# A two-layer decoder trunk on one core: q beside k, v of four heads and z of two groups as matmuls with 512 moving columns

## The chip, the cores and the metric

The kernel runs on one core of one Trainium2 chip. The metric is the device time of one execution in microseconds (us).

## The reference

Two layers over 512 tokens of width 1024, in float32. Each layer is a half-weighted SwiGLU, a token mixer and a second half-weighted SwiGLU, each behind an RMS norm and added to `x`. Layer 0 mixes by causal attention of 8 heads of width 128 (blocks of 256 keys, so that at 512 tokens every past block is chosen), layer 1 by a Mamba-2 mixer of 8 groups with 4 heads each.

```
for i in range(2):
    x = x + 0.5 * swiglu(rms_norm(x), gate[i], up[i], down[i])     # 1024 -> 2816 -> 1024
    h = rms_norm(x)
    x = x + (attention(h) if i == 0 else mamba2(h))
    x = x + 0.5 * swiglu(rms_norm(x), gate2[i], up2[i], down2[i])

attention(h): q, k, v = h @ w_qkv                    # 1024 -> 3 * 1024
              q, k = rope(rms_norm(q) * gq), rope(rms_norm(k) * gk)   # norms per head
              o = softmax(causal(q k^T / sqrt(128))) v;  return o @ w_o
mamba2(h):    z, xbc, dt = h @ w_in;  xbc = silu(conv4(xbc));  y = ssd(xbc, dt) + d * xs
              y = group_rms_norm(y * silu(z));  return y @ w_out
```

## The kernel before

**Tiling.** `x` lies transposed in SBUF: 8 tiles of 128 features by 512 tokens. Every float32 operand is split into a high and a low part (`high`, on ACT, and `low`, on DVE), and `mm3` makes one product out of three matmuls: high by high, high by low, low by high. A weight comes in pieces of up to 128x2048 (`wraw`, four buffers, loaded by SP's queue), and `halve_weights` and `halve_low` turn each piece into units of 128x512 (`whi` on ACT, `wlo` on DVE, eight buffers of each).

**Shapes.** In the feed-forward parts, the mixer's `pin` and the output projections the weight is stationary and 512 tokens move. q, k and v of attention and the mixer's z are made token-major instead: 128 tokens of `h` (`xhi`, `xlo`) are stationary and the weight's columns move. `token_major` (L751) does so with 256 columns (two heads) and puts two token tiles side by side into one bank of PSUM; the mixer's loop at L1022 does the same for z of one group.

**Stages.** `attention` (L600) has four passes `c` of two heads, each with a piece for q, k and v (`wqkv[c, what]`). `roped` (L622) takes one bank: squares on ACT, the power -0.5 on POOL, the scaling and the sine product `ropeb` on DVE, the cosine product and the sum `ropea` on POOL, four transposes `ptr` on PE, and the halves `qkhi`, `qklo`. `head` (L661) makes scores `psc`, the softmax, transposes `ppt` and the product with v `po`; `project` (L725) adds the output projection `pwo`. `rope_tables` (L568) makes the sines and cosines; `prepare` spawns it at the start of attention. `mamba` (L793) runs its groups one after the other: `conv_tile` (`pin`), four `chunk`s of 128 tokens (`pxt`, `py`, `pst`), z (`pz`, gated by `gate`), `gated_norm` (transposes `pyt`, halves `yhi`, `ylo`) and, after groups 2, 4 and 7, a projection `pout`.

**Order.** Each of these is a Python generator that hands its instructions to `Scheduler` (L137). It keeps a planned clock for each engine, gives every instruction a planned length (`Op.cost`), and always issues the one that can begin first; `main` (L1076), which holds the big matmuls, comes last where several can. The result is one fixed list for each engine, and on the chip each engine works its list off in order. `pieces` (L332) lists the weights in the order of use, with planned times that set when a unit is halved.

Of the kernel before, what the change touches and what calls it, by code (L numbers as in the profile page):

```python
# [17 lines left out]
FR = mybir.dt.float32r  # L18
# [18 lines left out]
FIRST = (("w", 0), ("x", 0), ("x", 1), ("w", 1), ("x", 2), ("x", 3), ("w", 2), ("x", 4), ("x", 5), ("w", 3), ("x", 6), ("x", 7))  # L37

# [246 lines left out]
def trunk(ctx, tc, xT, pos, consts, cols, rows, wgu, wd, wqkv, wo, win, wdt, wout, outT):  # L285
# [48 lines left out]
    def piece(src, n, us):  # L334

        pieces.append((src, n, us))

    for l in range(2):
        for i in (2 * l, 2 * l + 1):
            if i == 1:  # L340
                for c in range(4):
                    for w in range(3):
                        if c == 3 and w == 2:
                            piece(wo[0], 2048, 1.36)
                        piece(wqkv[c, w], 2048, 0.72)
                for c in range(1, 4):
                    piece(wo[c], 2048, 1.36)
            if i == 3:
                piece(wdt, 256, 1.36)
                for g in range(G):  # L350
                    piece(win[g, 0], 2048, 2.73)
                    piece(win[g, 1], 2048, 2.73)
                    piece(win[g, 2], 2048, 0.72)
                    if g in (2, 4, 7):
                        for o in range(2):
                            piece(wout[{2: 0, 4: 1, 7: 2}[g], o], 2048, 2.73)
                for o in range(2):
                    piece(wout[3, o], 2048, 2.73)
            for hf in range(2):
                for j in range(HALF):  # L360
                    piece(wgu[i, hf * HALF + j], 2048, 2.73)
                for n in range(KT):
                    piece(wd[i, hf, n], HALF * 128, 2.73)
    length = {0.72: 11.5, 1.36: 5.5, 2.73: 10.9}
    raws, begun, units = {}, {}, {}
    needed, at = [], 0.0
    for src, n, us in pieces:
        needed.append(at)
        at += length[us] * n / 2048 if us != 0.72 else 11.5
    used = [0]  # L370

    def load_weights():
        for p in range(1, len(pieces)):
            src, n, _ = pieces[p]
# [130 lines left out]

    def residual(n, ps, scale, done):
# [7 lines left out]
    def ffn(i, nrm, done):  # L514
# [16 lines left out]
        for hf in range(2):  # L531
            h = {}
# [35 lines left out]
    def rope_tables():  # L568
        posf = yield tiny("posf", TT)
        yield V.tensor_copy(posf, posi)  # L570
        big = yield [slot(nm) for nm in ("ang", "angq", "sin", "cos")]
        ang, q, s, c = (b[:, :256] for b in big)
# [15 lines left out]
        for nm, g in (("q", q_gain), ("k", k_gain)):  # L588
            ta, tb = yield [slot(nm + o) for o in ("cos", "sin")]
            ta, tb = (t.rearrange("p (i d) -> p i d", d=128) for t in (ta, tb))  # L590
            for o in range(2):
                same = g[:, None, 64 * o:64 * o + 64].to_broadcast([128, TT, 64])
                other = g[:, None, 64 - 64 * o:128 - 64 * o].to_broadcast([128, TT, 64])
                yield GP.tensor_tensor(ta[:, :, 64 * o:64 * o + 64], c.rearrange("p (i d) -> p i d", d=64), same, op=OP.mult)
                yield GP.tensor_tensor(tb[:, :, 64 * o:64 * o + 64], s.rearrange("p (i d) -> p i d", d=64), other, op=OP.mult)
            op = GP.tensor_scalar(tb[:, :, 0:64], tb[:, :, 0:64], -1.0, None, op0=OP.mult)
            yield op.frees(big[2], big[3]) if nm == "k" else op
            tabs.append((ta, tb))

    def attention(nrm, done):  # L600
# [6 lines left out]
        heads_left = [2] * 4  # L607
# [14 lines left out]
        def roped(ps, i0, what, dst, ready, last):  # L622
# [11 lines left out]
            def heads(t):  # L634
                return t.rearrange("p (n d) -> p n d", d=128)

            def pairs(t):
                return t.rearrange("p (i h d) -> p i h d", i=2, d=128)

            yield V.tensor_tensor(heads(a), heads(ps), rstd[:, :, None].to_broadcast([128, 4, 128]), op=OP.mult).frees(ps, rstd, ss)  # L640
            yield When(lambda: len(tabs) > what)
            ta, tb = tabs[what]
            for o in range(2):
                yield V.tensor_tensor(pairs(b)[:, :, :, 64 * o:64 * o + 64], pairs(a)[:, :, :, 64 - 64 * o:128 - 64 * o],
                                      tb[:, i0:i0 + 2, None, 64 * o:64 * o + 64].to_broadcast([128, 2, 2, 64]), op=OP.mult)
            op = GP.tensor_tensor(pairs(a), pairs(a), ta[:, i0:i0 + 2, None, :].to_broadcast([128, 2, 2, 128]), op=OP.mult)
            yield op.frees(ta, tb) if last else op
            yield GP.tensor_tensor(a, a, b, op=OP.add).frees(b)
            pt = yield bank("ptr")
            ops = [PE.transpose(pt[:, 256 * h + 128 * i:256 * h + 128 * i + 128],  # L650
                                a[:, 256 * i + 128 * h:256 * i + 128 * h + 128], ident) for h in range(2) for i in range(2)]
            ops[-1].frees(a)
            yield ops
            for h in range(2):
                yield high(pt[:, 256 * h:256 * h + 256], dst[h][0][:, 128 * i0:128 * i0 + 256])
            for h in range(2):
                op = low(pt[:, 256 * h:256 * h + 256], *cut(dst[h], 128 * i0, 128 * i0 + 256))
                yield op.frees(pt) if h else op
            ready.append(dst)

        def head(n, h, tr, ready, vs):  # L661
            yield When(lambda: len(ready) == 4)
            qT, kT = tr[0][h], tr[1][h]
# [45 lines left out]
            for j in range(TT):  # L709
                b, o = place[j]  # L710
                ops += mm3(po[:, 128 * j:], cut(vs[j], 128 * h, 128 * h + 128), cut(ph[b], o, o + 128 * (TT - j)),
# [3 lines left out]
            heads_left[n // 2] -= 1  # L715
            if not heads_left[n // 2]:
# [26 lines left out]
        def values(ps, i0, vs):  # L743
            for o in range(2):
                hi, lo = yield [half_slot("vhi", FR), half_slot("vlo", FR)]
                yield high(ps[:, 256 * o:256 * o + 256], hi, nrm.r[:, i0 + o:i0 + o + 1])
                op = low(ps[:, 256 * o:256 * o + 256], hi, lo, nrm.r[:, i0 + o:i0 + o + 1])
                yield op.frees(*([ps] if o else []))
                vs[i0 + o] = (hi, lo)

        def token_major(p, i0, nm, final):  # L751

            ps = yield bank(nm)
            for o in range(2):
                for k in range(KT):
                    yield unit(p, k // 2)
                    yield When(lambda: nrm.h[k] is not None)
                    un = units[p][k // 2]
                    ops = mm3(ps[:, 256 * o:256 * o + 256], cut(nrm.h[k], 128 * (i0 + o), 128 * (i0 + o) + 128),
                              cut(un, 256 * (k % 2), 256 * (k % 2) + 256), k == 0, k == KT - 1)  # L760
                    if i0 and o:
                        if k % 2:
                            ops[-1].frees(*un)
                        if final:
                            ops[-1].frees(*nrm.h[k])
                    yield ops
            return ps

        for c in range(4):
            tr, ready, vs = [], [], {}  # L770
            for what in range(3):
                if c == 3 and what == 2:
                    yield from project(0, False)
                p = take(wqkv[c, what])
                if what < 2:
                    pairs_ = []
                    for _ in range(2):
                        pair = yield [slot("qkhi", FR), slot("qklo", FR)]
                        pairs_.append(pair)
# [387 lines left out]
```

## Time and profile before

| | |
|---|---|
| median of 3 runs | 2129.7 us (2129.24 to 2130.9) |
| the profiled execution, its own time | 2130.55 us |
| its span in the trace | 2128.7 us |
| TensorE (PE) busy | 2119.5 us |
| VectorE (DVE) busy | 1121.3 us |
| ScalarE (ACT) busy | 881.9 us |
| GpSimd (POOL) busy | 408.0 us |
| read from HBM | 199.89 MB |

The span runs from the first instruction to the last one; the execution's own time is 1.85 us longer. A busy time is the union of an engine's instructions. A matmul's row lasts from its start to its modelled end and overlaps the next one, so the pace of a row of matmuls is read from the distance of their starts, or from the length of a chain piece divided by its count.

### The profile page before, as it was taken

What the parts mean: (1) busy time and instruction counts of PE and PEld (TensorE: products, weight loads), DVE (VectorE), ACT (ScalarE), POOL (GpSimd) and SP (SyncE); (2) the same over time, 40 slices, a digit from 0 to 9 for tenths busy, and PEclk for the clock granted to TensorE, in tenths of its full rate; (3) what the DMA queues carried; (4) which work ended last, traced back from release to release, by engine and by line L of the source; (5) the groups of instructions that cost most, each with busy time, mean ns of one, the idle gap of its engine ahead of it and who ended that gap; (6) DMA issues with size and microseconds to landing.
All of it is one profiled execution on the core that took longest, in us unless ns stands there. A gap on an engine that the chain in (4) does not pass through costs nothing.

```text
span 2128.7 us, 27344 instructions
## 1 busy us (share of the span) xinstructions
PE 2119.5 (100%) x10660; PEld 1800.9 (85%) x10660; DVE 1121.3 (53%) x1881; ACT 881.9 (41%) x1690; POOL 408.0 (19%) x369
## 2 busy tenths in 40 slices
PE   9999999999999999999999999999999999999999
PEld 7888888999878888888888888888888888888887
DVE  6443444777764434444443444577675775443442
ACT  5322334454443323333332334774757744322331
POOL 1100111423231001111100111353343432100110
PEclk9999999999999999999999999999999999999999
DMA  6223223211222232232223223333333332232221
GB/s 228 80 101 106 93 82 113 80 60 60 99 80 87 82 119 99 69 119 99 81 95 112 93 82 115 72 109 105 94 102 97 99 102 97 81 107 100 93 87 48
DMA packets 37137, 203.80 MB, mean 96 GB/s; under 512 B 4240, under 2 KB 4880, under 8 KB 19728
## 3 DMA queue, kind: packets, MB, share of 16 engines
q1 hardware_dynamic: 37008, 202.07, 28.5%
q8 instruction: 83, 1.36, 0.3%
q14 instruction: 46, 0.38, 0.1%
HBM read 199.89 MB, written 2.16 MB: 95 GB/s over the span
## 4 chain that ended last, share of the span: by engine, by line
PE 98%; DVE 1%; POOL 0%; ACT 0%; DMA 0%; issue 0%; SPq 0%; POOLq 0%; ACTq 0%
PE pd L208 22%; PE pg L208 22%; PE pu L208 22%; PE pin L208 8%; PE pqkv L208 6%; PE pz L208 4%; PE pout L208 4%; PE pwo L208 2%; PE py L208 2%; PE psc L208 1%; PE pxt L208 1%; PE po L208 1%; PE pst L208 1%; PE ppt L208 0%; PE ptr L208 0%; PE pyt L208 0%
## 5 line engine op out<-in xcount | busy, mean ns | idle before, releaser
L208 DVE TENSOR_TENSOR wlo<-wraw,whi 128x512 fp32r<-128x512 f32 (+1 forms) x737 | 557.1, 763 | 678.9 <-ACT whi L208 671.2
L208 ACT ACTIVATE whi<-wraw 128x512 fp32r<-128x512 f32 (+1 forms) x737 | 452.8, 619 | 792.3 <-PE pd L208 281.1
L208 POOL TENSOR_TENSOR ga<-ga,rb 128x512 f32<-128x512 f32 x88 | 114.2, 1298 | 1051.8 <-ACT ga L208 644.4
L208 PE MATMUL pg<-xhi,whi 128*128 128x512 f32 x704 | 274.8, 390 | 1.3 <-ACT xhi L208 1.3
L208 PE MATMUL pg<-xlo,whi 128*128 128x512 f32 x704 | 274.8, 390 | 0.3 <-DVE xlo L208 0.3
L208 PE MATMUL pg<-xhi,wlo 128*128 128x512 f32 x704 | 274.6, 390 | 0.0
L208 PE MATMUL pu<-xhi,whi 128*128 128x512 f32 x704 | 274.3, 390 | 0.0
L208 PE MATMUL pu<-xhi,wlo 128*128 128x512 f32 x704 | 273.9, 389 | 0.0
L208 PE MATMUL pu<-xlo,whi 128*128 128x512 f32 x704 | 273.9, 389 | 0.0
L208 PE MATMUL pd<-hhi,whi 128*128 128x512 f32 x704 | 273.9, 389 | 0.0
L208 PE MATMUL pd<-hhi,wlo 128*128 128x512 f32 x704 | 273.9, 389 | 0.0
L208 PE MATMUL pd<-hlo,whi 128*128 128x512 f32 x704 | 273.9, 389 | 0.0
L208 PEld LDWEIGHTS pg<-xhi,whi 128*128 128x128 f32 x704 | 132.6, 188 | 29.1 <-ACT xhi L208 1.6
L208 PEld LDWEIGHTS pg<-xlo,whi 128*128 128x128 f32 x704 | 132.5, 188 | 28.4 <-DVE xlo L208 0.9
L208 PEld LDWEIGHTS pg<-xhi,wlo 128*128 128x128 f32 x704 | 132.5, 188 | 27.4
L208 PEld LDWEIGHTS pd<-hhi,whi 128*128 128x128 f32 x704 | 132.2, 188 | 27.5
L208 PEld LDWEIGHTS pu<-xhi,wlo 128*128 128x128 f32 x704 | 132.2, 188 | 27.4
L208 PEld LDWEIGHTS pd<-hlo,whi 128*128 128x128 f32 x704 | 132.2, 188 | 27.4
L208 PEld LDWEIGHTS pu<-xlo,whi 128*128 128x128 f32 x704 | 132.2, 188 | 27.4
L208 PEld LDWEIGHTS pu<-xhi,whi 128*128 128x128 f32 x704 | 132.2, 188 | 27.3
L208 PEld LDWEIGHTS pd<-hhi,wlo 128*128 128x128 f32 x704 | 132.2, 188 | 27.3
L208 ACT ACTIVATE hhi<-ga 128x512 fp32r<-128x512 f32 x88 | 55.6, 632 | 151.4 <-DVE ga L208 151.4
(210 smaller groups left out, 3408.1 us busy)
## 6 DMA issues: line engine op xcount, KB each, us to landing
wraw<-wgu SPq DMA_DIRECT2D x87, 1024.0 KB, 4.9
wraw<-wd SPq DMA_DIRECT2D x64, 704.0 KB, 4.1
wraw<-win SPq DMA_DIRECT2D x24, 1024.0 KB, 4.9
wraw<-wqkv SPq DMA_DIRECT2D x12, 1024.0 KB, 4.9
rows_b<-rows_d SPq DMA_DIRECT2D x32, 256.0 KB, 5.3
wraw<-wout SPq DMA_DIRECT2D x8, 1024.0 KB, 4.9
wraw<-wo SPq DMA_DIRECT2D x4, 1024.0 KB, 4.9
x<-xT SPq DMA_DIRECT2D x8, 256.0 KB, 6.1
```

Of the source, the lines that this page charges most:

```text
L208: op.fn(*op.args, **op.kw)
```

## The change

A helper `wide` takes two weight pieces and makes all 512 tokens of one output of 512 columns: for each pair of token tiles it opens two banks of PSUM, and for each of eight slices of 128 features it runs both token tiles against the same unit. It is used for q and k of two heads side by side (`wqk[c]`, four times), for v of four heads (`wv[c]`, twice) and for z of two groups (`wz[n]`, four times). `ATTN` and `SSM` list the order of the pieces. `roped` now takes one token tile with q and k of two heads, `columns` waits until all four token tiles of a pass are turned and makes 4 x 4 transposes, `values` and `gate` work on 512 columns, and `rope_tables` (now laid out by token pairs, in half slots) is spawned when the second half of the first feed-forward part begins. The host packs the weights to match.

```diff
+ATTN = (("qk", 0), ("v", 0), ("qk", 1), ("qk", 2), ("wo", 0), ("qk", 3), ("v", 1), ("wo", 1), ("wo", 2), ("wo", 3))
+
+SSM = (("x", 0), ("z", 0), ("x", 1), ("x", 2), ("z", 1), ("out", 0), ("x", 3), ("x", 4), ("z", 2), ("out", 1),
+       ("x", 5), ("x", 6), ("x", 7), ("z", 3), ("out", 2), ("out", 3))
...
+    def wide(w, nrm, name, use, final):
+
+        ps_ = [take(w[0]), take(w[1])]
+        for i0 in (0, 2):
+            ps = yield [bank(name) for _ in range(2)]
+            for k in range(KT):
+                p = ps_[k // 4]
+                yield unit(p, k % 4)
+                yield When(lambda: nrm.h[k] is not None)
+                un = units[p][k % 4]
+                for o in range(2):
+                    i = i0 + o
+                    ops = mm3(ps[o], cut(nrm.h[k], 128 * i, 128 * i + 128), un, k == 0, k == KT - 1)
+                    if i == TT - 1:
+                        ops[-1].frees(*un)
...
+                    yield ops
+            for o in range(2):
+                use(ps[o], i0 + o)
...
+            if hf and midway:
+                midway()
...
-            yield from rope_tables()
...
+        def roped(ps, i, turned):
...
-            yield [V.tensor_scalar(ss[:, 2 * o:2 * o + 2], ss[:, 2 * o:2 * o + 2], 1.0 / DH, eps_ms[:, i0 + o:i0 + o + 1],
-                                   op0=OP.mult, op1=OP.add) for o in range(2)]
+            yield V.tensor_scalar(ss, ss, 1.0 / DH, eps_ms[:, i:i + 1], op0=OP.mult, op1=OP.add)
...
             yield GP.tensor_tensor(a, a, b, op=OP.add).frees(b)
-            pt = yield bank("ptr")
...
+            turned[i] = a
+
+        def columns(turned, tr, last):
+
+            yield When(lambda: len(turned) == TT)
...
             for h in range(2):
+                for w in range(2):
+                    pt = yield bank("ptr")
+                    ops = [PE.transpose(pt[:, 128 * i:128 * i + 128], turned[i][:, 256 * w + 128 * h:256 * w + 128 * h + 128], ident)
+                           for i in range(TT)]
...
+                    yield ops
+                    pair = yield [slot("qkhi", FR), slot("qklo", FR)]
+                    yield high(pt, pair[0])
+                    yield low(pt, *pair).frees(pt)
+                    tr[w, h] = pair
...
+        for what, c in ATTN:
+            if what == "wo":
+                yield from project(c, c == 3)
+            elif what == "v":
+                yield from wide(wv[c], nrm, "pv", lambda ps, i: spawn(values(ps, i, values_of[c])), c == 1)
+            else:
+                turned, tr = {}, {}
+                spawn(columns(turned, tr, c == 3))
+                for h in range(2):
+                    spawn(head(2 * c + h, h, tr, values_of[c // 2]))
+                yield from wide(wqk[c], nrm, "pqk", lambda ps, i: spawn(roped(ps, i, turned)), False)
...
-            yield When(lambda: c // 2 in box["z"])
...
+            yield When(lambda: (g // 2, c) in zs)
...
+            yield S.activation(z, ps, AF.Silu, scale=nrm.r[:, i:i + 1]).frees(ps)
...
+        yield from ffn(0, norms[0], norms[1].add, lambda: spawn(rope_tables(), EASY - 1))
```

**PE in attention, before**: the first piece of v around the transposes of q's first token pair (`whi`, `wlo`: moving weights; `xhi`, `xlo`: stationary tokens; `cc`: the identity; the numbers tell tiles apart).

```order
L208 MATMUL pqkv_3116<-whi_2927,xhi_2551 128x256
L208 MATMUL pqkv_3116<-wlo_2928,xhi_2551 128x256
L208 MATMUL pqkv_3116<-whi_2927,xlo_2552 128x256
L208 MATMUL ptr_3110<-cc_80,ropea_3020 128x128 x4
L208 MATMUL pqkv_3116<-whi_2937,xhi_2607 128x256
L208 MATMUL pqkv_3116<-wlo_2938,xhi_2607 128x256
L208 MATMUL pqkv_3116<-whi_2937,xlo_2608 128x256
```

**And now**: the end of the first piece of v, where the transposes of the first piece of q and k stand.

```order
L214 MATMUL pv_3098<-whi_2999,xhi_2823 128x512
L214 MATMUL pv_3098<-wlo_3000,xhi_2823 128x512
L214 MATMUL pv_3098<-whi_2999,xlo_2824 128x512
L214 MATMUL ptr_3181<-cc_80,ropea_2933 128x128
L214 MATMUL ptr_3181<-cc_80,ropea_3038 128x128
L214 MATMUL ptr_3181<-cc_80,ropea_3085 128x128
L214 MATMUL ptr_3181<-cc_80,ropea_3110 128x128
L214 MATMUL pv_3099<-whi_2999,xhi_2823 128x512
L214 MATMUL pv_3099<-wlo_3000,xhi_2823 128x512
L214 MATMUL pv_3099<-whi_2999,xlo_2824 128x512
L214 MATMUL pqk_3208<-whi_3115,xhi_2428 128x512
```

Four transposes that need one turned token pair stood in the stream after v's first matmuls. Now the first four stand behind 93 of v's 96 matmuls and need all four turned tiles (`ropea`).

**DVE in attention, before**: the sine products `ropeb` of that token pair, and what stands ahead of them.

```order
L208 SCALAR_TENSOR_TENSOR rs_a_2922<-rs_a_2922,rstd_2921 128x4
L208 SCALAR_TENSOR_TENSOR rstd_2921<-rs_a_2922,rstd_2921 128x4
L208 TENSOR_TENSOR ropea_3020<-pqkv_2774,rstd_2921 128x512
L208 TENSOR_TENSOR wlo_2928<-wraw_2578,whi_2927 128x512
L208 TENSOR_TENSOR wlo_2938<-wraw_2578,whi_2937 128x512
L208 TENSOR_TENSOR wlo_2951<-wraw_2578,whi_2950 128x512
L208 TENSOR_TENSOR ropeb_3021<-ropea_3020,qsin_2877 128x4x64 x2
```

**And now**: those of the last token tile of the first q and k.

```order
L214 SCALAR_TENSOR_TENSOR rs_a_3060<-rs_a_3060,rstd_3059 128x4
L214 SCALAR_TENSOR_TENSOR rstd_3059<-rs_a_3060,rstd_3059 128x4
L214 TENSOR_TENSOR ropea_3110<-pqk_2893,rstd_3059 128x512
L214 SCALAR_TENSOR_TENSOR vlo_3095<-pv_3001,r_2854,vhi_3094 128x512
L214 SCALAR_TENSOR_TENSOR vlo_3097<-pv_3002,r_2854,vhi_3096 128x512
L214 TENSOR_TENSOR wlo_3116<-wraw_2747,whi_3115 128x512
L214 TENSOR_TENSOR wlo_3128<-wraw_2747,whi_3127 128x512
L214 TENSOR_TENSOR wlo_3139<-wraw_2747,whi_3138 128x512
L214 TENSOR_TENSOR ropeb_3111<-ropea_3110,ropesin_1587 128x4x64 x2
L214 TENSOR_TENSOR wlo_3150<-wraw_2747,whi_3149 128x512
```

The three `wlo` ahead of the last sine products halve units 0 to 2 of the next q and k piece, and their buffers come free in the second token pair of v: between the last matmul there that reads unit 2 and the transposes above, 27 matmuls of v stand in PE's list.

**PE at the end of the mixer, before**: the last three of group 7's transposes `pyt`, in the midst of projection 2.

```order
L208 MATMUL pyt_15270<-cc_80,y_15138 128x128
L208 MATMUL pyt_15270<-cc_80,y_15165 128x128
L208 MATMUL pyt_15270<-cc_80,y_15194 128x128
L208 MATMUL pout_15267<-yhi_13704,whi_15000 128x512
L208 MATMUL pout_15267<-ylo_13705,whi_15000 128x512
L208 MATMUL pout_15267<-yhi_13704,wlo_15001 128x512
L208 MATMUL pout_15267<-yhi_14305,whi_15000 128x512
L208 MATMUL pout_15267<-ylo_14306,whi_15000 128x512
L208 MATMUL pout_15267<-yhi_14305,wlo_15001 128x512
L208 MATMUL pout_15267<-yhi_14322,whi_15000 128x512
```

**And now**:

```order
L214 MATMUL pyt_14260<-cc_80,y_14185 128x128
L214 MATMUL pyt_14261<-cc_80,y_14059 128x128
L214 MATMUL pyt_14261<-cc_80,y_14149 128x128
L214 MATMUL pyt_14261<-cc_80,y_14179 128x128
L214 MATMUL pyt_14261<-cc_80,y_14185 128x128
L214 MATMUL pout_14258<-yhi_14145,whi_14015 128x512
L214 MATMUL pout_14258<-ylo_14146,whi_14015 128x512
L214 MATMUL pout_14258<-yhi_14145,wlo_14016 128x512
L214 MATMUL pout_14258<-yhi_14276,whi_14015 128x512
L214 MATMUL pout_14258<-ylo_14277,whi_14015 128x512
L214 MATMUL pout_14258<-yhi_14276,wlo_14016 128x512
L214 MATMUL pout_14258<-yhi_14285,whi_14015 128x512
```

Before, 21 matmuls of projection 2 stood between the last `pyt` and projection 3, which alone reads their result. Now projection 3 has begun ahead of them, and the first matmul that reads the new halves (`yhi_14276`) comes three matmuls after the last transpose.

## Rows read from the trace of the kernel before

**Rows 1.** The page: span, busy shares, clock slices, chain that ended last.
```profile
span 2128.7 us, 27344 instructions
...
PE 2119.5 (100%) x10660; PEld 1800.9 (85%) x10660; DVE 1121.3 (53%) x1881; ACT 881.9 (41%) x1690; POOL 408.0 (19%) x369
...
PEclk9999999999999999999999999999999999999999
...
PE 98%; DVE 1%; POOL 0%; ACT 0%; DMA 0%; issue 0%; SPq 0%; POOLq 0%; ACTq 0%
```

**Rows 2.** Chain that ended last: start us, us, what.
```profile
130.30 59.84 PE pd L208 x264
...
1358.18 11.51 PE pz L208 x96
```

**Rows 3.** Matmul groups by shape, whole span: busy us, mean ns, idle before.
```profile
L208 PE MATMUL pd<-hhi,whi 128*128 128x512 f32 x704 | 273.9, 389 | 0.0
...
L208 PE MATMUL pqkv<-whi,xhi 128*128 128x256 f32 x384 | 110.6, 288 | 0.0
...
L208 PE MATMUL pz<-whi,xhi 128*128 128x256 f32 x256 | 73.9, 289 | 0.0
```

**Rows 4.** The longest waits of PE, by releaser: us, times, longest us.
```profile
PE ptr L208 <- POOL ropea L208: 1.7, 2, 0.9
PE pg L208 <- ACT xhi L208: 1.3, 1, 1.3
...
PE po L208 <- DVE ptlo L208: 0.3, 1, 0.3
```

**Rows 5.** PE in order of time at one wait of a transpose: start us, us.
```profile
411.01 0.28 PE L208 MATMUL pqkv<-wlo,xhi 128*128 128x256 f32 x1
411.13 0.28 PE L208 MATMUL pqkv<-whi,xlo 128*128 128x256 f32 x1
412.24 0.66 PE L208 MATMUL ptr<-cc,ropea 128*128 128x128 f32 x4 [0.83 <-POOL ropea L208]
```

**Rows 6.** Busy time by stretch (attention, mixer, feed-forward); columns as in the first line.
```profile
core 0: us, PE busy (x) PEld busy (x) DVE busy (x) ACT busy (x) POOL busy (x), PEclk, DMA share, GB/s
369.66:607.00 237.34, 235.00 (x1723) 219.88 (x1723) 180.76 (x403) 120.14 (x353) 80.45 (x65) 1.00 0.21 72
1328.00:1765.00 437.00, 437.00 (x2539) 383.71 (x2538) 299.90 (x540) 278.33 (x545) 175.66 (x184) 1.00 0.32 97
190.00:310.00 120.00, 120.00 (x531) 99.41 (x530) 53.76 (x76) 40.04 (x66) 13.27 (x11) 1.00 0.26 89
```

**Rows 7.** Groups of ACT, DVE and POOL in the attention stretch.
```profile
L208 DVE TENSOR_TENSOR wlo<-wraw,whi 128x512 fp32r<-128x512 f32 x61 | 47.4, 801 | 1.6 <-ACT whi L208 1.6
L208 ACT ACTIVATE whi<-wraw 128x512 fp32r<-128x512 f32 x63 | 39.4, 631 | 38.6 <-PE pqkv L208 18.6 <-PE pwo L208 17.1 <-PE pd L208 1.4
...
L208 POOL TENSOR_TENSOR ropea<-ropea,ropeb 128x512 f32<-128x512 f32 x16 | 21.5, 1344 | 1.3
L208 POOL TENSOR_TENSOR rstd<-ssq,mhalf 128x4 f32<-128x4 f32 x16 | 19.3, 1206 | 42.1 <-DVE ssq L208 42.1
L208 ACT ACTIVATE junk<-pqkv 128x128 f32<-128x128 f32 x64 | 17.9, 279 | 10.1 <-PE pqkv L208 8.4
L208 ACT ACTIVATION_READ_ACCUMULATOR junk<-pqkv 128x1 f32 x64 | 12.8, 199 | 0.0
L208 POOL TENSOR_TENSOR ropea<-ropea,kcos 128x512 f32<-128x512 f32 x8 | 12.7, 1593 | 39.7 <-DVE ssq L208 18.5 <-PE pqkv L208 15.0 <-DVE ropeb L208 6.2
...
L208 DVE TENSOR_TENSOR ropea<-pqkv,rstd 128x512 f32<-128x512 f32 x16 | 11.0, 688 | 0.5
...
L208 DVE TENSOR_TENSOR ropeb<-ropea,qsin 128x256 f32<-128x256 f32 x16 | 6.2, 419 | 0.2
```

**Rows 8.** Two groups of the mixer stretch, by the same view.
```profile
L208 DVE SCALAR_TENSOR_TENSOR ylo<-pyt,colp,yhi 128x512 fp32r<-128x512 f32 x16 | 11.4, 744 | 7.6 <-ACT yhi L208 7.6
...
L208 ACT ACTIVATE yhi<-pyt,colp 128x512 fp32r<-128x512 f32 x16 | 10.3, 682 | 4.5 <-PE pyt L208 4.5
```

More of the change, by code (lines that the diff above doesn't have):

```diff
@@ L332, in trunk, with piece, wide_pieces @@
     pieces = []
-    def piece(src, n, us):
-        pieces.append((src, n, us))
+    def piece(src, n=2048, unit=2.73, total=None):
+        pieces.append((src, n, unit, unit * n / 512 if total is None else total))
+    def wide_pieces(w):
+        piece(w[0], unit=1.36)
+        piece(w[1], unit=1.36, total=16.4)
     for l in range(2):
@@ L587, in rope_tables, with four @@
         yield S.activation(c, ang, AF.Sin).frees(posf, big[0], big[1])
[L588 to L598, printed above, removed]
+        def four(t):
+            return t.rearrange("p (i w d) -> p i w d", i=2, d=128)
+        for n in range(2):
+            pair = yield [slot("ropecos"), slot("ropesin")]
+            ta, tb = map(four, pair)
+            cs_, sn = (t[:, 128 * n:128 * n + 128].rearrange("p (i d) -> p i d", d=64) for t in (c, s))
+            for w, g in ((0, q_gain), (1, k_gain)):
+                for o in range(2):
+                    same = g[:, None, 64 * o:64 * o + 64].to_broadcast([128, 2, 64])
+                    other = g[:, None, 64 - 64 * o:128 - 64 * o].to_broadcast([128, 2, 64])
+                    yield GP.tensor_tensor(ta[:, :, w, 64 * o:64 * o + 64], cs_, same, op=OP.mult)
+                    yield GP.tensor_tensor(tb[:, :, w, 64 * o:64 * o + 64], sn, other, op=OP.mult)
+            op = GP.tensor_scalar(tb[:, :, :, 0:64], tb[:, :, :, 0:64], -1.0, None, op0=OP.mult)
+            yield op.frees(big[2], big[3]) if n else op
+            tabs.append(pair)
     def attention(nrm, done):
@@ L620, in attention, with heads, four @@
         spawn(prepare(), 25)
-        def roped(ps, i0, what, dst, ready, last):
+        def heads(t):
+            return t.rearrange("p (n d) -> p n d", d=128)
+        def four(t):
+            return t.rearrange("p (w h d) -> p w h d", w=2, d=128)
+        def roped(ps, i, turned):
             yield When(lambda: "r" in state)
@@ L652, in roped @@
-            ops[-1].frees(a)
-            yield ops
-            for h in range(2):
[L655 to L663, printed above, removed]
+            turned[i] = a
@@ L741, in project @@
                 spawn(residual(n, ps, None, done if last else None), 5)
[L743 to L779, printed above, removed]
-                    tr.append(pairs_)
-                for i0 in (0, 2):
-                    ps = yield from token_major(p, i0, "pqkv", c == 3 and what == 2)
-                    if what < 2:
-                        spawn(roped(ps, i0, what, tr[what], ready, c == 3 and i0 == 2))
-                    else:
-                        spawn(values(ps, i0, vs))
-                if what == 1:
-                    for h in range(2):
-                        spawn(head(2 * c + h, h, tr, ready, vs))
@@ L790, in attention, with values @@
-        for c in range(1, 4):
-            yield from project(c, c == 3)
+        def values(ps, i, vs):
+            hi, lo = yield [slot("vhi", FR), slot("vlo", FR)]
+            yield high(ps, hi, nrm.r[:, i:i + 1])
+            yield low(ps, hi, lo, nrm.r[:, i:i + 1]).frees(ps)
+            vs[i] = (hi, lo)
+        values_of = {0: {}, 1: {}}
+        for what, c in ATTN:
+            if what == "wo":
+                yield from project(c, c == 3)
+            elif what == "v":
+                yield from wide(wv[c], nrm, "pv", lambda ps, i: spawn(values(ps, i, values_of[c])), c == 1)
+            else:
+                turned, tr = {}, {}
[3 more added lines that the diff above has]
+                yield from wide(wqk[c], nrm, "pqk", lambda ps, i: spawn(roped(ps, i, turned)), False)
@@ L886, in conv @@
             box[nm] = acc
-        ys = {}
+        ys, zs = {}, {}
+        zs_left = {(n, c): 2 for n in range(G // 2) for c in range(TT)}
         def chunk(g, c, box, chain):
@@ L1054, in mamba @@
-        yield from project(3, True)
+        for what, n in SSM:
+            if what == "x":
+                box = {"y": {}}
+                box["ss"] = yield tiny("yss", TT)
+                spawn(decays(n, box))
+                p = take(win[n, 0])
+                yield from conv_tile(p, 0, 16 + n, "b", box, False)
+                yield from conv_tile(p, 1, 24 + n, "c", box, False)
+                p = take(win[n, 1])
+                for o in range(2):
+                    yield from conv_tile(p, o, 2 * n + o, f"x{o}", box, n == G - 1 and o == 1)
+                chain = {}
+                for c in range(TT):
+                    spawn(chunk(n, c, box, chain))
+            elif what == "z":
+                yield from wide(wz[n], nrm, "pz", lambda ps, i: spawn(gate(ps, i, n)), n == G // 2 - 1)
+            else:
+                yield from project(n, n == 3)
```

154 lines of the change are left out of this document (62 added, 92 removed).

## The prediction

> **What bounds the kernel now.** I read the page first. TensorE is busy for 2119.5 of 2128.7 us, at a granted clock of nine tenths or more in each slice, and the chain that ended last lies on it for 98% [rows 1]. A busy PE need not be a fast one, since its rows overlap. So the next view is the chain itself, for the pace: 264 matmuls of 512 moving columns take 59.84 us, 226.7 ns each, and 96 of 256 columns take 11.51 us, 119.9 ns each [rows 2]. Two narrow ones cost 239.8 ns and do the work of one wide one. The differences give both parts: 256 more columns cost 106.8 ns, so what is left, 13.1 to 13.2 ns, is paid once for each matmul. The groups by shape say how many of the narrow kind there are: three groups of 384 for q, k and v, three of 256 for z [rows 3]. The list of waits then shows that little else can be gained: PE's longest sum of waits is 1.7 us, for two sets of transposes [rows 4]. Last, the windows show what the other engines have to spare: in attention DVE is busy for 180.76 of 237.34 us, in the mixer for 299.90 of 437, in the feed-forward part for 53.76 of 120 [rows 6]. DVE is the one to watch, and attention the place.
>
> **The narrow matmuls become wide.** Removed are 1152 + 768 = 1920 matmuls at 119.9 ns, 230.2 us [rows 2, 3]. Added are 960 at 226.7 ns, 217.6 us; the order list has them as `pqk`, `pv` and `pz` with 512 columns. All of it lies on PE, which never rests long: **-12.6 us**. The price of the wide kind is that of `pd`, where the weight is stationary; here the tokens are. Both operands have the same type and the same 128x128 and 128x512 shapes, so I take it unchanged. Its bounds are the nearest rows: not under 226.7, and not over two narrow ones, 239.8, at which nothing is won.
>
> The Trainium skill has a rule that speaks against this. Its page "TensorE: Matmul & The Clock Gate", section "Back-to-back issue gap", gives N / 2.4 + 2.5 ns between matmuls, so 109.2 ns for 256 columns and 215.8 for 512. By that rule the sum would be 209.6 - 207.1 = 2.5 us, an estimate from that page, in place of 12.6. The rows show 119.9 and 226.7, so the measured fixed part decides.
>
> **Waits that go.** One wait for transposes starts 1.11 us after the matmul ahead of it, where 0.12 is the pace: 0.99 us lost [rows 5]. The view of waits has two such, 1.7 us by the modelled ends [rows 4]; each modelled end lies 0.28 - 0.12 = 0.16 us past the next possible start, so 2.0 us in all. These sets stand elsewhere now: **-2.0 us** (0 to -2.0).
>
> **Waits that come in attention.** `columns` needs all four turned tiles, so there is one first set of transposes for each of the four q and k passes. For the first pass the order shows what decides. The last `ropeb` stands in DVE's list behind the halving of three units of the next piece, and the third of these must wait until PE has read unit 2 of v for the last time. From there PE has 27 matmuls of cover, 27 x 0.2267 = 6.1 us. The other side is one `whi` 0.63, one `wlo` 0.80, two `ropeb` 0.84, a cosine product 1.59 and a sum 1.34 on POOL, 5.2 us [rows 7], plus five hand-overs between engines, for which no row stands alone: at nothing the chain is 5.2 us, at a narrow matmul's 0.12 each it is 5.8, against 6.1. Just in time. The plan puts the first set of each pass where it believes the tiles ready, so each of the four is as tight. Bounds for each: 0, and about 1.5, half more than the wait seen before [rows 5]. I take 0.5, since the chain worked out above ends on the good side: **+2.0 us** (0 to 6).
>
> **A wait at the mixer's end.** After the last `pyt`, three matmuls of projection 3 (0.68 us) and the second half of the transposes are all the cover for group 7's halves; the order before had 21 matmuls more. The first half's transposes need ACT 0.68 and DVE 0.74 us [rows 8], 1.4 us; PE arrives about 1.1 us after them, and first reads the high half, which is there. The low half is read 0.23 us later: **+0.4 us** (0 to 1.5).
>
> **What I cost at nothing.** The transposes, scores, `po`, `pin` and `pout` keep their counts. The halves of v and q and k and the gates of z become half as many of double width, which saves DVE and ACT some fixed costs in a stretch where both have time to spare [rows 6]. If they filled it, the wait would show at `psc`. The sines and cosines move from the start of attention into the first feed-forward part, where DVE idles for 66 of 120 us and POOL for 107 [rows 6]. What covers them is the eight units halved ahead: one feeds 12 matmuls there, so eight are 8 x 12 x 0.2267 = 21.8 us of PE's work. If that cover failed, a unit would be late by one row of the longest kind moved, under 1.6 us [rows 7]. SP's queue loads as many pieces as before; those of z stand behind the `rows_b` loads that wait for older groups' chunks, which end more than a piece (21.8 us) earlier in PE's list.
>
> **Sum.** -12.6 - 2.0 + 2.0 + 0.4 = -12.2 us. The durations are from the profiled execution, whose own time is 2130.55 us with its span of 2128.7 [rows 1]; it gives 2118.35. The median of the runs is 0.85 us lower, so **2117.5 us**. Of this, 0.2% is 4.3 us, about what a measurement can tell from no change: faster means under 2125.4, slower over 2134.0.
>
> **The rivals.**
> - *More waits in attention.* DVE is at 76% there, works its list in order, and its list now has weight halves between the parts of a rope. If the first sets of transposes, the scores behind them and the projection wait for 4 to 8 us more in all, the time is 2121 to 2125.4. For: the near-zero slack above. Against: the plan of before missed PE's needs by 2 us in eight passes. Chance 0.16.
> - *Waits that eat the gain.* The same with 8 to 16 us more: 2125.4 to 2134.0, within 0.2%. Chance 0.07.
> - *The fixed part is not halved.* The 13 ns could belong to moving weights over stationary tokens, and come twice with twice the columns: then a wide matmul of this kind takes up to 239.8 ns [rows 2], nothing is won, and with the waits above the time is 2130.1; halfway, at 233.2 ns, it is 2123.8. Decided by the pace alone. Against it: `pd`, with 512 columns, and `pz`, with 256, have the same fixed part, whichever operand is the weight [rows 2]. I put the case at 235.5 ns or more, 2126 to 2130.1: chance 0.03. The Trainium skill's rule above would give 2127.6, an estimate from that page, inside this case.
> - *The barrier of four tiles.* Slower: a pass's transposes need the last pair of tiles, which end together, and if that pair's whole chain began behind the unit that PE frees, its second tile would need, after the first one's 1.21 + 1.59 + 1.34 = 4.1 us on POOL, its own four squares (1.9), power (1.2), scaling (0.7), two sine products (0.84), 1.59 and 1.34: 7.6 [rows 7]. That is 11.7 us against 6.1 of cover, 5.6 a pass, 22.4 in all, in place of the 2.0: 2130.55 - 12.6 - 2.0 + 22.4 + 0.4 - 0.85 = 2137.9 us. It decides for slower from a wait of about 4.7 us a pass. For: POOL serves the four tiles one after the other. Against: the list puts only the last `ropeb` behind these units. Chance 0.05.
> - *Better.* No new waits at all, and fewer switches between kinds of matmuls: 2111.5 to 2114.5. Chance 0.07.
> - That the change doesn't do what it says is not left: the order has the 512 columns.
>
> **How the numbers follow.** The forecast with its bounds, 2114.5 to 2121, has 0.62. Faster: 0.62 + 0.16 + 0.07 = 0.85; within 0.2%: 0.07 + 0.03 = 0.10; slower: 0.05. The range 2114.0 to 2123.5 holds the forecast's case, over half of the first rival and a little of the last, and leaves out some 0.2.
>
> **What would show it.** The chain's pieces of `pqk`, `pv` and `pz` should have 0.227 us a matmul; 0.2355 or more would be the third rival. The attention stretch should be shorter by some 7.5 us (576 x 13.1 ns) and the mixer's by 5 (384 x 13.1 ns). PE's waits for `ropea` at `ptr` should stay under 3 us, none over 1.5. A wait of 4 us or more there is the barrier; waits at `psc` for `qklo`, or at `pqk` for `whi`, are DVE's list. The forecast is wrong if the wide pace holds and the total still misses by over 4 us.

## The result, and the profile after

The changed kernel takes 2116.83 us, against 2129.76 us before: a ratio of 0.9937, with an interval of 0.9918 to 0.9957. One disturbed run is left out. The forecast was 2117.5 us, and faster. A second comparison, made later with the last experiments, gave 2115.82 against 2129.43, 0.9935 [0.9921, 0.9949]. The gain is 12.9 to 13.6 us.

The page of the changed kernel, its first lines and the share of the chain by engine:

```profile
span 2113.9 us, 25353 instructions
...
PE 2106.1 (100%) x9700; PEld 1748.7 (83%) x9700; DVE 1117.0 (53%) x1841; ACT 877.6 (42%) x1650; POOL 400.4 (19%) x377
...
PE 98%; DMA 1%; DVE 0%; ACT 0%; SPq 0%; POOL 0%; issue 0%; ACTq 0%; POOLq 0%
```

PE has 960 matmuls fewer (10660 in [rows 1]) and is as full as before: still the bound, with 98% of the chain. So the time has gone out of PE's own work, and the chain that ended last must show where (start us, us, what):

```profile
309.37 59.84 PE pd L214 x264
...
442.82 21.83 PE pqk L214 x96
...
1677.72 15.69 PE pz L214 x69
```

`pd` has the old pace, 226.7 ns [rows 2]. The new kinds take 21.83 / 96 = 227.4 ns and 15.69 / 69 = 227.4, where two narrow ones took 239.8. The 0.7 ns more lies at the head of such a piece, behind other matmuls. Further in, the pace is that of `pd`; between these two starts lie 45 steps, 10.20 us / 45 = 226.7 ns:

```profile
449.98 0.39 PE L214 MATMUL pqk<-whi,xlo 128*128 128x512 f32 x1
...
460.18 0.39 PE L214 MATMUL pqk<-whi,xlo 128*128 128x512 f32 x1
```

Whether anything new is waited for, PE's waits tell (us in total, times, longest us):

```profile
PE pg L214 <- ACT xhi L214: 1.2, 1, 1.2
PE warm L214 <- DVE warm L1054: 1.2, 1, 1.2
PE pg L214 <- DVE xlo L214: 0.5, 2, 0.3
PE ss L214 <- DVE acc L214: 0.5, 1, 0.5
...
PE pout L214 <- DVE ylo L214: 0.2, 1, 0.2
```

The 1.7 us for `ptr` that led [rows 4] are gone, as is the 0.3 of `po`, and nothing took their place there. All that is new in the stages rebuilt is the last row, 0.2 us at the mixer's end.

Next, the stretches that answer to [rows 6]; columns as there:

```profile
369.21:596.45 227.24, 227.01 (x1146) 188.98 (x1145) 168.92 (x350) 117.16 (x327) 68.76 (x54) 1.00 0.21 75
1318.00:1750.00 432.00, 431.80 (x2153) 363.24 (x2152) 301.02 (x540) 276.04 (x529) 170.81 (x184) 1.00 0.31 98
190.00:310.00 120.00, 120.00 (x531) 99.38 (x530) 58.42 (x87) 40.52 (x68) 22.30 (x29) 1.00 0.26 89
```

In attention DVE has 12 us less to do and POOL 12, in the feed-forward part DVE has 4.7 more and POOL 9.0: part of that is the tables' move (e5 below parts it), and PE is busy for 120.00 of 120 us there all the same.

The windows' edges are rounded. Exact lengths come from the first matmul of each stage, by the timeline of PE:

```profile
369.05 0.39 PE L214 MATMUL pqk<-whi,xhi 128*128 128x512 f32 x1
...
596.28 0.39 PE L214 MATMUL pg<-xhi,whi 128*128 128x512 f32 x1
...
1317.92 0.39 PE L214 MATMUL pdt<-xhi,whi 128*32 128x512 f32 x1
...
1749.56 0.39 PE L214 MATMUL pg<-xhi,whi 128*128 128x512 f32 x1
```

Attention is 596.28 - 369.05 = 227.23 us long and the mixer 1749.56 - 1317.92 = 431.64. The same four matmuls of the kernel before:

```profile
369.50 0.28 PE L208 MATMUL pqkv<-whi,xhi 128*128 128x256 f32 x1
...
606.51 0.39 PE L208 MATMUL pg<-xhi,whi 128*128 128x512 f32 x1
...
1328.16 0.39 PE L208 MATMUL pdt<-xhi,whi 128*32 128x512 f32 x1
...
1764.39 0.39 PE L208 MATMUL pg<-xhi,whi 128*128 128x512 f32 x1
```

So they were 237.01 and 436.23. Attention is shorter by 9.78 us, the mixer by 4.59, the time ahead of attention by 0.45, and the rest is the same to 0.02. This adds up to the spans' difference of 14.8 us. The medians differ by less: the profiled execution of before lies 0.8 us above its median and that of the changed kernel 0.9 below.

### The profile page after: what moved, and what is told of

It reads as the page before. It is cut to its first block, busy times and chain, and to the rows that moved or that the text cites. A ratio compares the mean times of both kernels' runs of the same rounds, so it can differ in the third digit from the quotient of the medians.

```text
span 2113.9 us, 25353 instructions
## 1 busy us (share of the span) xinstructions
PE 2106.1 (100%) x9700; PEld 1748.7 (83%) x9700; DVE 1117.0 (53%) x1841; ACT 877.6 (42%) x1650; POOL 400.4 (19%) x377
## 3 DMA queue, kind: packets, MB, share of 16 engines
q8 instruction: 76, 1.25, 0.2%
## 4 chain that ended last, share of the span: by engine, by line
PE 98%; DMA 1%; DVE 0%; ACT 0%; SPq 0%; POOL 0%; issue 0%; ACTq 0%; POOLq 0%
PE pd L214 23%; PE pu L214 22%; PE pg L214 22%; PE pin L214 8%; PE pqk L214 4%; PE pz L214 4%; PE pout L214 4%; PE pv L214 2%; PE pwo L214 2%; PE py L214 2%; PE psc L214 1%; PE pxt L214 1%; PE po L214 1%; PE pst L214 1%; PE ppt L214 0%; DMA wraw<-wgu 0%
```

## The experiments

**The theory**: the gain is the fixed 13 ns of 960 matmuls, and the order around them matters only where PE comes to wait. **The rivals**: the gain comes from the rebuilt order (fewer passes, tables elsewhere, other places for transposes), or from waits that went; and, of the waits, that their absence is a property of the new stages, or else of the plan that placed them.

The table has the stage lengths of each profiled execution, read like those above, and the medians. The lengths tell more than the medians do, as the start of the kernel alone varies by more than a microsecond (attention began between 368.30 and 369.67 us).

| kernel | attention us | mixer us | median us | ratio to before |
|---|---|---|---|---|
| before | 237.01 | 436.23 | 2129.76 | |
| changed | 227.23 | 431.64 | 2116.83 | 0.9937 [0.9918, 0.9957] |
| e1_narrow_all | 233.50 | 434.98 | 2125.71 | 0.9982 [0.9973, 0.9990] |
| e2_narrow_qkv | 233.47 | 431.66 | 2122.51 | 0.9969 [0.9957, 0.9981] |
| e3_narrow_z | 227.25 | 435.18 | 2119.49 | 0.9955 [0.9943, 0.9968] |
| e4_quarter | | | 2283.11 | 1.0721 [1.0706, 1.0736] |
| e5_tables_late | 227.54 | 431.74 | 2116.84 | 0.9939 [0.9927, 0.9951] |
| e6_z3_early | 227.16 | 438.22 | 2122.14 | 0.9963 [0.9949, 0.9977] |
| e7_pool_short | 241.61 | 432.11 | 2132.51 | 1.0013 [1.0004, 1.0022] |
| e8_before_pool_long | 234.93 | 436.74 | 2127.98 | 0.9990 [0.9981, 0.9999] |
| e9_spare | 227.20 | 431.51 | 2114.70 | 0.9930 [0.9917, 0.9942] |
| e10_after_again | 227.26 | 431.67 | 2115.82 | 0.9935 [0.9921, 0.9949] |

**Narrow again, in the new order: e1, e2, e3.** In the changed kernel's `wide`, each matmul of slices 1 to 6 of the eight becomes two of 256 columns; e2 does it for q, k and v alone, e3 for z alone (their `w` in the last two lines):

```diff
-                    ops = mm3(ps[o], cut(nrm.h[k], 128 * i, 128 * i + 128), un, k == 0, k == KT - 1)
+                    w = 256 if 0 < k < KT - 1 else 512
+                    h = cut(nrm.h[k], 128 * i, 128 * i + 128)
+                    ops = [op for e in range(0, 512, w) for op in mm3(ps[o][:, e:e + w], h, cut(un, e, e + w), k == 0, k == KT - 1)]
...
+                    w = (512 if name == "pz" else 256) if 0 < k < KT - 1 else 512
...
+                    w = (256 if name == "pz" else 512) if 0 < k < KT - 1 else 512
```

> The changed kernel with its own order and stages, but in wide() six of the eight feature slices run as two matmuls of 256 columns each (the first and the last slice stay 512 wide): 720 wide matmuls become 1440 narrow ones. Theory (a fixed 13.1 ns for each matmul): +720 x 13.1 ns = +9.4 us on the changed kernel, 2126.2 us, 0.9983 of the kernel before. Rival 1 (the gain came from the new order, the waits that went and the moved tables): no change, 2116.8 us, 0.994. Rival 2 (wide ones with stationary tokens are dearer than 226.7 ns): less than +9.4 us.

> As e1, but only for q, k and v: 432 wide matmuls become 864 narrow ones, z stays wide. Theory: +432 x 13.1 ns = +5.7 us on the changed kernel, 2122.5 us, 0.9966 of the kernel before, all of it in the attention stretch. Rival 1 (order and waits): 2116.8 us.

> As e1, but only for z: 288 wide matmuls become 576 narrow ones, q, k and v stay wide. Theory: +288 x 13.1 ns = +3.8 us on the changed kernel, 2120.6 us, 0.9957 of the kernel before, all of it in the mixer stretch. e2 and e3 should add up to e1. Rival 1 (order and waits): 2116.8 us.

All 720 split give back 8.9 us by the medians. The parts do so each in its own stage: splitting q, k and v (432 matmuls, 432 x 13.1 ns = 5.7 us) lengthens attention by 6.24 us and leaves the mixer alone; splitting z (288, 3.8 us) lengthens the mixer by 3.54 and leaves attention alone. In e1 and e2 attention also has one new wait, `pqk` for ACT's `p`: 1.2 us in the view of waits, 1.3 by the starts. Without it e2 shows (6.24 - 1.3) / 432 = 11.4 ns for each matmul split and e3 12.3, a little under the 13.1 of long runs. The chain of e1 shows the old pace (start us, us, what):

```profile
1354.50 17.05 PE pz L214 x126
```

Such a stretch holds both widths: 108 narrow ones at 119.9 ns and 18 wide ones at 227.4 give 17.04 us. What e1 keeps of the gain is accounted for too. Its mixer is 1.25 us shorter than before; the 96 matmuls of z left wide are worth 96 x 13.1 ns = 1.26, less 0.36 for the wait at the mixer's end. Its attention is 3.51 us shorter: 144 x 13.1 ns = 1.9 for those left wide, 2.1 for the waits at `ptr` that went (e8, below), and 0.6 for the wait of `po` in [rows 4], which went too (0.3 in the view, 0.6 by the starts, 592.22 and 593.05); together 4.6, less the 1.3 of the new wait. So, waits apart, the rebuilt order is worth some tenths of a microsecond in each stage at most, and the theory stands.

**Narrower still: e4.** The same edit with 128 columns, to see whether the straight line of the two widths goes on.

```diff
+                    w = 128 if 0 < k < KT - 1 else 512
```

> As e1, but the six slices run as four matmuls of 128 columns each: 720 wide matmuls become 2880. If the cost is a straight line in the columns (13.1 ns and 0.417 ns a column), one takes 66.5 ns: +720 x (4 x 66.5 - 226.7) = +28.3 us, 2145 us. If there is a floor near the 0.11 us at which the 128-column matmuls of po follow each other in the trace of before, +720 x (4 x 110 - 226.7) = +154 us, 2270 us.

The line doesn't go on: the second case of the expectation, the floor, came near. From PE's timeline of e4, at two places:

```profile
384.82 0.41 PE L214 MATMUL pqk<-whi,xhi 128*128 128x128 f32 x1
...
385.25 0.41 PE L214 MATMUL pqk<-whi,xlo 128*128 128x128 f32 x1
...
499.82 0.27 PE L214 MATMUL pqk<-whi,xhi 128*128 128x128 f32 x1
...
500.04 0.28 PE L214 MATMUL pqk<-whi,xlo 128*128 128x128 f32 x1
```

Between the rows of each pair lies one matmul more. In the second pair, at the full clock, the starts are 0.11 us apart, hardly nearer than the 0.1199 of 256 columns; the line had 0.067. 2880 such matmuls in place of 720 wide ones cost 2880 x 0.1105 - 720 x 0.227 = 155 us, so 2272. The other 11 us show in the first pair: starts 0.21 apart, at half the clock. That was not expected and has a part of its own below. For this kernel it says that 13.1 ns is a difference between 256 and 512 columns, and no price that holds for every width. One thing stays open: each matmul has a weight load of its own (PE and PEld have the same counts on the page), so that the change took away loads as well as matmuls, and PEld fell from 219.88 us [rows 6] to 188.98 in attention. In the narrow `pz` of the kernel before, from 1358.2 to 1369.6 us, PEld is busy for all of the 11.40 us. The loads alone don't set the 119.9 ns, as e4 has one every 110.5; whether the 13.1 ns belong to the matmul or to its load, no run here separates.

**The tables back in attention: e5.**

```diff
-        yield from ffn(0, norms[0], norms[1].add, lambda: spawn(rope_tables(), EASY - 1))
+        yield from ffn(0, norms[0], norms[1].add)
...
             yield V.tensor_copy(neg_b, neg)
+            yield from rope_tables()
```

> The changed kernel with the sine and cosine tables made at the start of attention again, as in the kernel before (in the new layout). Theory (DVE and POOL have room there, the first transposes come 21 us after the first q and k): within 0.5 us of the changed kernel, 2116.8 us. Rival (moving the tables gave part of the gain): 1 to 3 us slower, with a wait for ropea at ptr or for acc at ss in the first pass.

The median is that of the changed kernel, and attention is 0.3 us longer by the first matmuls. The windows (columns as in [rows 6]) show that the work did move back:

```profile
190.00:310.00 120.00, 120.00 (x531) 99.42 (x530) 53.77 (x76) 39.90 (x66) 13.10 (x11) 1.00 0.26 89
369.50:597.00 227.50, 226.92 (x1146) 188.92 (x1145) 178.15 (x364) 116.88 (x328) 75.63 (x72) 1.00 0.21 75
```

DVE is at 178 of 227 us in attention, and PE has one wait there that the changed kernel doesn't have, 0.6 us for DVE's `x` in the projection (`pwo`); whether the tables cause it isn't shown. The tables' place is worth 0.3 us in attention and nothing in the median.

**Group 3's z one step earlier at the mixer's end: e6.** This gives up part of what covers group 7's last tiles.

```diff
-       ("x", 5), ("x", 6), ("x", 7), ("z", 3), ("out", 2), ("out", 3))
+       ("x", 5), ("x", 6), ("z", 3), ("x", 7), ("out", 2), ("out", 3))
```

> The changed kernel with the last piece of z ahead of group 7's x, b and c instead of behind them. Theory: the wait of PE for ylo in projection 3 (0.36 us by the starts in the changed kernel) goes and nothing else changes, 2116.4 us. Rival: group 7's chunks now come later against the projections, their chain up to pyt has less cover, and a new wait of 1 us or more stands ahead of py or pyt: 2117.5 us or more.

The theory's expectation was wrong here, and the rival's right. PE's timeline (in brackets the idle time ahead and what ended it) and a window of e6:

```profile
1730.35 1.74 PE L214 MATMUL pyt<-cc,y 128*128 128x128 f32 x8 [2.79 <-DVE y L214]
1732.24 0.80 PE L214 MATMUL pout<-yhi,whi 128*128 128x512 f32 x1 [0.15 <-ACT yhi L214]
...
1735.33 0.63 PE L214 MATMUL pout<-yhi,whi 128*128 128x512 f32 x1
1735.75 0.63 PE L214 MATMUL pout<-ylo,whi 128*128 128x512 f32 x1
...
1738.59 0.40 PE L214 MATMUL pout<-yhi,wlo 128*128 128x512 f32 x1
```
```profile
1734.00:1736.00 2.00, 2.00 (x6) 1.56 (x5) 0.43 (x1) 0.63 (x1) 0.00 (x0) 0.50 0.00 0
```

The wait for group 7's `y` is 2.8 us, and it costs more than its length. Behind it the granted clock is 0.50, and 14 starts from 1732.24 to 1738.59 take 6.35 us where 14 x 0.2275 = 3.2 would do; the eight transposes take 1.0 us more than in the changed kernel, for most of which the granted clock is still 1.00, so that its cause stays open. With the 2.8, and less the 0.36 lost there by the changed kernel itself, this is 6.6 us, which is the mixer's difference in the table. The medians differ by 5.3 (from 2116.84, the kernel of the same comparison that has the same mixer).

**Is the missing wait in attention luck of the plan? e7 and e8.** The planner's cost of a POOL operation on 512 elements is 0.185 + 0.00216 x 512 = 1.29 us. The trace has 1.59 for the cosine product and 1.34 for the sum [rows 7]. In e7 the changed kernel is planned with 0.4 of this cost, in e8 the kernel before with 1.3 of it; the instructions are the same, only the order follows.

```diff
-            return 0.62 if wide else 0.185 + 0.00216 * n
+            return 0.62 if wide else (0.185 + 0.00216 * n) * (0.4 if n == 512 else 1.0)
```

> The changed kernel, same instructions, but the planner takes POOL's operations of 512 columns for 0.52 us in place of 1.29, so it places the transposes, and all that waits for such operations, earlier than the tiles are ready. Theory (the waits at ptr are the error of the plan, and the plan leaves no slack): two such operations close each rope, 1.5 us too early, so about 1 to 2 us of wait at each of the four first sets, +4 to +8 us, 2121 to 2125 us; more if the feed-forward parts wait too. Rival (there was slack of its own in the new order): no waits at ptr, 2117 us.

> The kernel before, same instructions, but the planner takes POOL's operations of 512 columns for 1.68 us in place of 1.29. Theory (the two waits at ptr before were the error of the plan): they go, -2.0 us, 2127.7 us, 0.9991 of the kernel before. Rival (they belong to the narrow structure with two q and k banks a pass): the two waits stay, 2129.8 us.

The first row is from the waits of e7, the next ones from PE's timeline, with what was waited for in brackets:

```profile
PE ptr L214 <- POOL ropea L214: 9.5, 4, 3.3
```
```profile
404.44 0.49 PE L214 MATMUL ptr<-cc,ropea 128*128 128x128 f32 x3
408.22 0.48 PE L214 MATMUL ptr<-cc,ropea 128*128 128x128 f32 x1 [3.28 <-POOL ropea L214]
...
409.35 0.63 PE L214 MATMUL pv<-whi,xlo 128*128 128x512 f32 x1
409.77 0.63 PE L214 MATMUL pv<-whi,xhi 128*128 128x512 f32 x1
```

With a plan that thinks POOL fast, one set of transposes in each of the four passes waits, for the fourth tile as the rival of four tiles had it (three transposes go at 404.44, the fourth at 408.22). The waits are 3.28, 3.29, 0.39 and 2.56 us, 9.5 in all, but attention is 14.4 us longer than in the changed kernel and the median 15.7: after the three longer ones the matmuls start 0.43 us apart for 2.6 to 2.8 us, so the clock is halved again. The whole gain is gone, and a little more. The expectation, 2121 to 2125, had the waits at 4 to 8 us and counted nothing behind them.

e8 is the counterpart. In its view of waits `ptr` no longer stands, and its attention is 234.93 us, 2.08 shorter than before (its mixer is 0.51 longer). So the two waits before were an error of the plan of about 2 us, which the kernel before could have been rid of without any wide matmul.

**More room in the plan: e9, beside the changed kernel again: e10.** `SPARE` is the time that the planner keeps free ahead of a need.

```diff
-SPARE = 0.25
+SPARE = 0.6
```

> The changed kernel, same instructions, but the planner holds back each of PE's small sets (transposes, scores, py, pst) by 0.6 us in place of 0.25 after it believes their operands ready; the order then changes between big and small sets of PE 613 times against 626. Theory (the waits that the plan can remove are nearly all gone, PE is bound by the number and the width of its matmuls): within 1 us of the changed kernel, 2116 to 2118 us. Rival (small waits that hide in the starts are still worth something): 2 us or more faster.

> The changed kernel itself once more, beside e9 and against the kernel before, for a closer interval: 2116.8 us, 0.994 of the kernel before, by every theory.

(The counts in the expectation of e9 are of the planned lists; no trace shows them.) It is the fastest version run: 2114.56 to 2114.96 in five runs, against 2115.30 to 2116.69 for the changed kernel on the same chip, 1.1 us by the medians, between the theory's 1 and the rival's 2. But attention and mixer are the same to 0.16 us. The first matmul of attention starts at 368.30 in place of 369.35, so the difference lies nearly all ahead of it. The first matmul of the feed-forward part and the fourth, e9's and then e10's:

```profile
6.05 0.52 PE L214 MATMUL pg<-xhi,whi 128*128 128x512 f32 x1
...
7.41 0.40 PE L214 MATMUL pg<-xhi,whi 128*128 128x512 f32 x1
```
```profile
6.73 0.50 PE L214 MATMUL pg<-xhi,whi 128*128 128x512 f32 x1 [1.67 <-ACT xhi L214]
...
8.53 0.63 PE L214 MATMUL pg<-xhi,whi 128*128 128x512 f32 x1
```

e10 waits 1.67 us for the first `xhi` and reaches the fourth matmul 1.12 us later than e9; from there its starts are 0.43 us apart for a while, against 0.23. e9 has no such wait and no such stretch in this execution. The changed kernel's first profile has a wait of 1.23 us there and no slow matmuls. Whether `SPARE` does this, or what happens in the first microseconds, stays open.

## Why the prediction was right

The total was right, and in the main for the reason given; one term was mis-sized, and part of the closeness is luck. Step by step:

- **"The narrow matmuls become wide", -12.6 us.** Right. The step that decided it, that the price of `pd` holds where tokens are the weight, held: inside long pieces the pace is 226.7 ns. Over whole stages the width gave a little less, about 12 us: 9.78 - 2.1 - 0.6 = 7.1 in attention and 4.59 + 0.36 = 4.95 in the mixer. The Trainium skill, page "TensorE: Matmul & The Clock Gate", section "Back-to-back issue gap", gives N / 2.4 + 2.5 ns as the gap of an isolated matmul; by it the gain would have been 960 x 2.5 ns = 2.4 us, an estimate from that page (2.5 by the prediction's rounded terms). e2 and e3 take back some 4.9 and 3.5 us with three quarters of the matmuls, so that rule doesn't describe this stream. The word "fixed" went too far: that 13.1 ns is paid for each matmul was worked out from two widths, and e4 shows that it doesn't hold at a third.
- **"Waits that go", -2.0 us.** Right. e8, in which the kernel before keeps its matmuls and loses these waits, shortens attention by 2.08 us.
- **"Waits that come in attention", +2.0 us (0 to 6).** Mis-sized: it measured 0. The chain was counted at 5.2 to 5.8 us against 6.1 of cover, and it did end just in time: `ropea` of the fourth tile is finished 0.36 us before the transposes start. From POOL's and PE's timelines of the changed kernel:

```profile
409.10 1.70 POOL L214 TENSOR_TENSOR ropea<-ropea,ropecos 128x512 f32<-128x512 f32 x1 [5.08 <-DVE ropeb L214]
410.87 1.62 POOL L214 TENSOR_TENSOR ropea<-ropea,ropeb 128x512 f32<-128x512 f32 x1
```
```profile
412.62 0.40 PE L214 MATMUL pv<-whi,xlo 128*128 128x512 f32 x1
412.85 0.60 PE L214 MATMUL ptr<-cc,ropea 128*128 128x128 f32 x4
```

  410.87 + 1.62 = 412.49, and PE takes the first `ptr` at 412.85, 0.23 us after the matmul ahead of it: no time lost. What failed is the step from a small slack to a wait. The half microsecond a pass was chosen from a chain that by its own sum ended in time; the sum should have been believed, and the risk left to the range. Nor is "each of the four as tight": by the same rows of the other passes the fourth tile is ready 2.0, 0.5 and 4.2 us ahead. In the four passes PE waits nowhere for `ropea`. That it could have gone otherwise is shown by e7.
- **"A wait at the mixer's end", +0.4 us (0 to 1.5).** Right, and at the place named. PE's timeline:

```profile
1728.66 0.39 PE L214 MATMUL pout<-yhi,whi 128*128 128x512 f32 x1
1729.25 0.50 PE L214 MATMUL pout<-ylo,whi 128*128 128x512 f32 x1 [0.20 <-DVE ylo L214]
```

  The high half is there when PE comes; for the low half the start is 0.59 us after the one before in place of 0.23, 0.36 us lost. The size is partly luck: the terms as written, 1.4 us against 1.1 + 0.23, give 0.1, and nothing was said of the other 0.3.
- **"What I cost at nothing".** Right to some tenths. e5 moves the tables, and the median stays; PE's feed-forward window is full; no wait at `psc` or at `pz` is listed. What it missed is on the good side, the 0.6 us at `po`.

By stage: the mixer was to be 5 us shorter less the 0.4, and is shorter by 4.59. Attention was to be 7.5 shorter with waits that cancel, and is shorter by 9.78. Its q, k and v matmuls, each counted from its start to the next one's, took 142.1 us before and take 133.1 now: 9.1 us, of which 2.1 are the two waits and 7.0 the width. The rest is mainly the wait at `po`. So the profiled execution shows 14.65 us in place of 12.2: 2.0 more by the mis-sized term, 0.45 by the start of the kernel, and the 0.6 at `po` against the half microsecond that the width gave less. The medians show 12.9 to 13.6. That the forecast is only 0.7 us off the first of them is in part luck, since the missing waits were offset by where the two profiled executions lie among their runs.

Of the rivals, "Better" came true in its mechanism for attention (no new wait there), with a time above its 2111.5 to 2114.5. "More waits in attention" and "The barrier of four tiles" are excluded by the view of waits, and e7 shows that they were real possibilities: four sets late by 9.5 us in all, and the time 15.7 us worse. Their prices left out the clock. "The fixed part is not halved" is excluded by the pace. What was held against it beforehand, that `pd` and `pz` have the same fixed part, was no evidence, since the 13.1 ns had been worked out from these two by taking them for points of one line.

## What to carry to other kernels

Where PE is full, count matmuls as well as columns, and read the price of each width from the distance of their starts in a long run of the same kind; two widths give a fixed part, but only between them (a third width fell off the line). A plan written from costs is as good as the costs: compare them with the trace's durations, as an operation planned at 0.4 of its cost lost the whole gain. Price a wait of PE of some 3 us at more than its length, because the matmuls behind it can run at half the clock.

## What the runs showed of the hardware

**The clock fell at waits of 2.6 to 3.3 us, and cost time behind them.** After 2.79 us without a matmul (e6) the granted clock was 0.50 until about 1738.3 us, and wide matmuls started 0.43 us apart: 1.2 in place of 2.4 GHz. These starts cost 3.2 us more than at the full clock. After 3.28, 3.29 and 2.56 us (e7) the same, but for a shorter time; there attention lost 14.4 us with 9.5 us of waits. The wait of 0.83 us in the kernel before [rows 5] and the 0.20 us at the mixer's end show nothing of this: the windows around them have 1.00. At the very start it goes both ways: after 1.67 us e10 runs slowly, after 1.23 us the first profile of the changed kernel does not, and after 1.31 us the kernel before does, with six steps of 0.427 us between these two rows of its timeline:

```profile
7.65 0.63 PE L208 MATMUL pg<-xhi,wlo 128*128 128x512 f32 x1
...
10.21 0.63 PE L208 MATMUL pg<-xhi,wlo 128*128 128x512 f32 x1
```

So the profiled execution of before has a slow stretch of its own, some 1.5 us of lost time, which that of the changed kernel has not; attention begins only 0.45 us later there all the same.

**It also fell without a wait.** From the windows of e4, columns as in [rows 6]:

```profile
370.00:376.00 6.00, 6.00 (x51) 5.82 (x50) 2.06 (x5) 1.47 (x3) 2.38 (x2) 1.00 0.52 175
376.00:380.00 4.00, 4.00 (x23) 4.00 (x22) 0.47 (x4) 0.00 (x0) 0.00 (x0) 0.55 0.00 0
380.00:386.00 6.00, 6.00 (x30) 6.00 (x30) 0.00 (x0) 0.00 (x0) 0.00 (x0) 0.50 0.00 0
...
398.00:402.00 4.00, 4.00 (x16) 3.30 (x16) 0.23 (x1) 1.73 (x10) 0.20 (x1) 0.72 0.00 0
...
470.00:522.00 52.00, 52.00 (x438) 50.88 (x437) 16.58 (x38) 11.63 (x42) 15.06 (x12) 1.00 0.15 54
```

PE is busy throughout, with matmuls of 128 columns 0.11 us apart since 374.56, and from about 376.4 the clock is halved until about 400. The same kind of matmuls runs from 470 to 522 us at the full clock, among them some of 512 columns. What made the one stretch different was not tried. It cost 102 such matmuls x 0.10 and five of 512 columns x 0.20, 11 us, near what e4 exceeds its sum by.

**Below 256 columns a matmul costs nearly the same.** 128 columns take 0.1105 us and 256 take 0.1199. The Trainium skill, page "TensorE: Matmul & The Clock Gate", section "Back-to-back issue gap", also has a sustained figure for a stream of weight loads and matmuls, about 81 ns at 128 columns and 131 at 512; the rows here, 110.5 and 226.7, agree with neither.
